# Start of a hybrid decoder step: one load for c and the bound parameters ahead of the first weight piece, and two VectorE steps moved behind the shift's columns

## The chip, the cores and the metric

The kernel runs on one core of a Trainium2 chip. The metric is the device time in microseconds (us) of one execution; a kernel's time is the median of its runs. The engines are TensorE (PE, with its weight loads as PEld), VectorE (DVE), ScalarE (ACT), GpSimd (POOL) and SyncE (SP), which here only issues DMAs.

## What is computed

One inference step of a decoder layer, for a prompt of 512 positions and 8 sample tokens (T = 520 columns), with a model width of 1024 (KO = 8 blocks of 128). What matters here is its beginning:

```
cs  = silu(c)                                  # c: 9 vectors of 1024 (1 prompt, 8 samples)
sh1, sc1, g1, sh2, sc2, g2 = split(cs @ w_mod + b_mod, 6)
h   = rmsnorm(x, norm1_g) * (1 + sc1) + sh1
u   = h @ w_in                                 # 8 groups of 1024 columns
lb, decay = functions of hg_lower and lru_lambda ("bound parameters")
```

After that follow the HGRN2 and RG-LRU recurrences over u, the gated merge, an output projection, and a second modulated norm with a feed-forward block.

## The kernel before

All matrix products run on TensorE with the weights stationary. A weight tile of 1024 x 128 is loaded as `wst`, rounded by ScalarE to the high part `whi`, and VectorE forms the low part `wlo = wst - whi`; activations `h` are kept as a high and a low part in the same way. `products` (L156) takes high x high, high x low and low x high for each block k and each half of 260 columns: six products per block, 48 per weight tile. `gemm` (L170) postpones the low weight part of the first four blocks until the fourth, so `wlo` is needed only after 16 products.

`begin` (L1718) is written out by hand and its TensorE, ScalarE and VectorE instructions keep the order in which they are written (class `InOrder`); what is issued without it is placed by a scheduler that works from a model of the times. It goes like this:

1. Loads. ScalarE's queue issues `c9` (the vectors c, L348) and `pl` (the bound parameters, L288). SyncE's queue issues the first 1 MB piece of the scale weights (`wm`, from `w_piece`), `xT0`, `pm` (`params_mod`, with b_mod and the norm gains, L1758), `xT1`, `raw` (the first three weight tiles, in four parts), `xsr`, the next piece, and so on. A load that reuses one of eight load semaphores waits for the load that had it.
2. `zeros(4)` (L1737): eight instructions of products of zeros on TensorE.
3. `cond` (L355): ScalarE's exponential of c and three VectorE steps give `cT` = silu(c). VectorE then adds 1 to two groups of columns of `pm`, starts on the bound parameters (`bounds`), ScalarE takes their exponentials and loads the table for the square root.
4. `piece(0)`: TensorE multiplies cT with the first piece; ScalarE copies the result (`modev`), TensorE turns it into columns, VectorE makes `modT`, the scale (it needs `pm`). `zeros(1)` and `zeros(3)` stand around this.
5. `high` (ScalarE) and `low` (VectorE) make the first scaled blocks of h; TensorE starts on the first three weight tiles, block by block, while three more pieces are multiplied in. The norm's root is applied afterwards: `rs` holds it per position.
6. `rooted` (L1819) multiplies each block of x by scale and root on VectorE; `evict` (L1871) multiplies a finished tile by the root on its way out of PSUM; `mod_rows` and `mod_cols` (L367, L382) multiply cT with the shift weights and give the shift's columns `shp`. From `shp` on, `high_again` and `low_again` make the final h (x with root, scale and shift), TensorE multiplies the shift into the first three tiles (`pw`), and the ordinary weight tiles begin, with the low part of their first tile made by `_split_w` (L109).

In step 6 VectorE's list reads: rooted blocks 0 to 3, the low part of the first ordinary weight tile, evict(0), rooted 4 and 5, evict(1), rooted 6 and 7, `shp`, then the low parts of h.

Of the kernel before, what the change touches and what calls it, by code (L numbers as in the profile page):

```python
# [6 lines left out]
F32 = mybir.dt.float32  # L7
# [4 lines left out]
OP = mybir.AluOpType  # L12
# [8 lines left out]
KO = D // 128  # L21
# [22 lines left out]
NM = 9  # L44
# [37 lines left out]
class Kernel:  # L82
    def __init__(self, ctx, tc, ins, outs):
        self.ctx, self.tc, self.nc = ctx, tc, tc.nc
        self.i, self.o = ins, outs
        self.start_act = self.gate_last = self.rows_last = None
        self.group, self.sigmoids, self.mod_open, self.lo_after = None, [], None, None


# [19 lines left out]
    def _split_w(self, st, place, after=None):  # L109
        if place is None:  # L110
            hi, lo = (self.wst.tile([128, KO, 128], F32R, tag="wst", name=n) for n in ("whi", "wlo"))
        else:
            pool = self.sw if place % 2 else self.whl
            hi, lo = (pool.tile([128, KO, 128], F32R, tag=f"{n}{place}", name=n, bufs=1) for n in ("whi", "wlo"))
        ins = self.nc.scalar.copy(hi, st)  # L115
        if after or self.start_act:
            self.behind(ins, after or self.start_act)
        with self.urgent():
            self.wlo = self.nc.vector.tensor_tensor(lo, st, hi.bitcast(F32), OP.subtract)  # L119
        self.whi = ins  # L120
        if self.lo_after:
            self.behind(ins, self.rounded)
            self.behind(self.wlo, self.lo_after)
            self.lo_after = None
        return hi, lo
# [156 lines left out]
    def load_parameters(self):  # L282
# [3 lines left out]
        self.gcol = self.pm[:, 70:72]  # L286
        self.pl = self.start.tile([128, 16], F32, name="pl")
        self.nc.scalar.dma_start(self.pl, self.i["params_bound"])  # L288
        self.pa = t = self.hc.tile([128, 313], F32, name="pa")
# [53 lines left out]
    def load_c(self):  # L343
        nc = self.nc
        self.act0 = self.consts.tile([1, 1], F32, name="act0")
        nc.vector.memset(self.act0, 0.0)
        self.c9 = self.start.tile([128, KO, NM], F32, name="c9")
        nc.scalar.dma_start(self.c9, self.i["c"])  # L348
        self.cT = self.hc.tile([128, KO, 32], F32, name="cT")
# [1368 lines left out]
    def begin(self):  # L1718
# [17 lines left out]

        zeros(4)  # L1737
        xsr, fs, fsh = (self.start.tile([128, KO, NB], F32, name=n) for n in ("xsr", "fs", "fsh"))
# [18 lines left out]
        self.load_x(0)  # L1757
        nc.sync.dma_start(self.pm, self.i["params_mod"])  # L1758
        self.load_x(1)
# [157 lines left out]
        rows = [load_wide("w_rows", i) for i in range(4)]  # L1917
        self.load_after = self.wide
        self.ready_w(-AHEAD, 1)
# [5 lines left out]
        evict(0)  # L1925
        rooted(4, 5)
        evict(1)
        rooted(6, 7)
        for k in range(4, KO):
            self.mod_rows(psh, k, rows[k])  # L1930
        ev = self.mod_out(psh)
        products((0,), 6, 7, tiles=(2,))
        self.mod_cols(0, self.shp[:, :, :NM], ev)
        products((1, 2), 6, 7, tiles=(2,))
        pw = pb()
# [6 lines left out]
        for i in range(KO // 2):  # L1942
# [3 lines left out]
            if i == 1:  # L1946
                nc.scalar.copy(sw, pw[:, :FIRSTS * 128])
        evict(2)
        self.last_product = nc.tensor.last
# [96 lines left out]
def layouts(i):  # L2046
# [11 lines left out]
        "xs": x[:, :, L:].transpose(1, 0, 2).reshape(128, KO * NB),  # L2058
        "c": c.T.reshape(KO, 128, NM).transpose(1, 0, 2),
        "params_mod": np.concatenate([columns(i[n]) for n in ("b_mod", "norm1_g", "norm2_g", "final_norm_g")], 1),  # L2060
        "params_bound": np.concatenate([columns(i[n]) for n in ("hg_lower", "lru_lambda")], 1),
        "params": np.concatenate([columns(i[n]) for n in ("hg_onorm_g", "lru_conv_w",
# [50 lines left out]
```

## Time and profile before

| what | us |
|---|---|
| median of 3 runs | 994.23 (993.11 to 994.47) |
| the profiled execution | 994.33 |
| its span in the trace | 992.5 |
| PE busy in the span | 979.6 |
| VectorE, ScalarE busy | 677.3, 540.2 |

The profiled execution took 994.33 us, of which the trace covers 992.5. In the timeline each line is one instruction or a run of equal ones: start, time, engine, line, operation, output<-inputs, count, and in brackets how long the engine had been idle before it and what released it. Helper lines show as L74, because the ordered engines are called through that line. PEclk is the granted TensorE clock as a share of full speed. SPq, ACTq are the issuing queues.

### The profile page before, as it was taken

How to read it: one execution, taken by the hardware profiler on the slowest of the kernel's cores; microseconds unless marked ns; L12 is line 12 of the kernel's file. 1: busy time of each engine (PE TensorE's matmuls, PEld its weight loads, DVE VectorE, ACT ScalarE, POOL GpSimd, SP SyncE). 2: the span in 40 equal slices, each digit the busy share in tenths (PEclk: the TensorE clock that was granted, in tenths of full speed). 3: DMA queues.
4: the chain of work that ended last, by engine and by line, in shares of the span. 5: the costliest groups of instructions: out<-in, count | busy, mean ns of one | idle time of the engine just before them, and what ended most of it. 6: DMA issues, size and time to landing. Idle time of an engine off the chain costs nothing.

```text
span 992.5 us, 23168 instructions
## 1 busy us (share of the span) xinstructions
PE 979.6 (99%) x9638; PEld 955.1 (96%) x9638; DVE 677.3 (68%) x1294; ACT 540.2 (54%) x1020; POOL 137.9 (14%) x252
## 2 busy tenths in 40 slices
PE   8999999999999999999999999999999999999997
PEld 6899999999999999999999999999999999999997
DVE  5884866675585658868635557767677766768685
ACT  4585746745664663456512233566456545646663
POOL 1410000000000101111100000012311331232050
PEclk8999999999999999999999999999999999999999
DMA  9653253343343425337556566322752572273242
GB/s 365 241 171 132 84 183 105 103 171 99 99 129 134 140 94 203 128 135 275 170 170 239 166 236 217 113 75 66 189 147 68 111 190 83 57 187 77 65 85 87
DMA packets 49001, 143.67 MB, mean 145 GB/s; under 512 B 6256, under 2 KB 15920, under 8 KB 47864
## 3 DMA queue, kind: packets, MB, share of 16 engines
q1 hardware_dynamic: 37008, 123.32, 36.7%
q0 software_dynamic: 11456, 18.70, 8.5%
q8 instruction: 75, 1.23, 0.5%
q14 instruction: 30, 0.25, 0.1%
q10 hardware_dynamic: 432, 0.18, 0.1%
HBM read 123.65 MB, written 11.26 MB: 136 GB/s over the span
## 4 chain that ended last, share of the span: by engine, by line
PE 92%; ACT 2%; DVE 2%; DMA 2%; issue 0%; SPq 0%; DVEq 0%; ACTq 0%
PE mm L165 62%; PE ps L1226 9%; PE pt L1226 4%; PE mm L931 2%; PE pb L1226 2%; PE pt L370 2%; PE ps L589 1%; PE ps L931 1%; PE pb L735 1%; DMA wm<-in_w_rows_dram 1%; DMA xT<-in_xT_dram 1%; PE pt L679 1%; PE pt L666 1%; PE pb L931 1%; DMA c<-in_c_dram 1%; PE mm L74 1%
## 5 line engine op out<-in xcount | busy, mean ns | idle before, releaser
L165 PE MATMUL mm<-h,whi 128*128 128x260 f32 (+1 forms) x2720 | 426.4, 285 | 0.0
L165 PEld LDWEIGHTS mm<-h,whi 128*128 128x128 f32 x2720 | 368.0, 188 | 1.6 <-issue 0.6
L119 DVE TENSOR_TENSOR wlo<-wst,whi 128x1024 fp32r<-128x1024 f32 x156 | 190.6, 1222 | 143.7 <-ACT whi L115 135.8
L165 PE MATMUL mm<-h,wlo 128*128 128x260 f32 x1360 | 255.9, 285 | 0.0
L115 ACT CAST whi<-wst 128x1024 fp32r<-128x1024 f32 x156 | 163.5, 1049 | 134.0 <-PE mm L165 106.5
L165 PEld LDWEIGHTS mm<-h,wlo 128*128 128x128 f32 x1360 | 202.1, 189 | 0.7 <-issue 0.2
L1321 POOL TENSOR_TENSOR ft<-ft,fsh 128x8 f32<-128x8 f32 x28 | 18.5, 660 | 210.3 <-DVE ft L1315 210.3
L1329 DVE TENSOR_TENSOR f<-f 128x260 f32<-128x260 f32 x64 | 27.3, 427 | 27.9 <-ACT f L1324 27.2
L1318 ACT ACTIVATE ft<-ft,fsh 128x512 f32<-128x512 f32 (+2 forms) x36 | 24.0, 675 | 36.0 <-DVE ft L1315 36.0
L244 POOL TENSOR_SCALAR ss<-ss 128x4 f32<-128x4 f32 x8 | 1.9, 233 | 284.6 <-ACT g L687 284.6
L165 PE MATMUL mm<-a,whi 128*128 128x260 f32 x256 | 37.5, 284 | 0.0
L165 PE MATMUL mm<-oa,whi 128*128 128x260 f32 x256 | 37.4, 283 | 0.0
L165 PE MATMUL mm<-b,whi 128*128 128x260 f32 x256 | 37.3, 283 | 0.0
L165 PEld LDWEIGHTS mm<-oa,whi 128*128 128x128 f32 x256 | 33.4, 188 | 0.8 <-issue 0.8
L165 PEld LDWEIGHTS mm<-a,whi 128*128 128x128 f32 x256 | 33.3, 188 | 0.8 <-issue 0.8
L165 PEld LDWEIGHTS mm<-b,whi 128*128 128x128 f32 x256 | 33.4, 188 | 0.4 <-issue 0.4
L603 DVE TENSOR_TENSOR X<-X,tb 128x512 f32<-128x512 f32 x48 | 30.9, 684 | 2.3 <-PE ps L589 1.3
L1363 POOL DMA_DIRECT2D ma<-snap x28 | 25.8, 934 | 41.9 <-issue 32.7
L1345 POOL DMA_DIRECT2D ma<-snap x28 | 26.0, 928 | 36.4 <-DMA ma<-snap 21.1
L1324 ACT ACTIVATE f<-ft 128x520 f32<-128x520 f32 (+1 forms) x36 | 20.7, 587 | 15.0 <-POOL ft L1322 13.0
L504 ACT ACTIVATE st<-st,fkq 128x128 f32<-128x128 f32 x64 | 20.0, 390 | 11.5 <-DMA st<-in_state_hgrn_dram 7.7
L192 ACT ACTIVATE gate<-pb,pa 128x260 f32<-128x260 f32 x32 | 15.4, 481 | 19.4 <-PE pb L735 19.4
(564 smaller groups left out, 2060.8 us busy)
## 6 DMA issues: line engine op xcount, KB each, us to landing
wst<-in_w_ff_dram SPq DMA_DIRECT2D x64, 512.0 KB
wst<-in_w_in_dram SPq DMA_DIRECT2D x53, 512.0 KB
wst<-in_w_mod_dram SPq DMA_DIRECT2D x32, 512.0 KB
wm<-in_w_piece_dram SPq DMA_DIRECT2D x4, 1024.0 KB
wm<-in_w_rows_dram SPq DMA_DIRECT2D x4, 1024.0 KB
st<-in_state_hgrn_dram SPq DMA_DIRECT2D x8, 512.0 KB
vb<-vd SPq DMA_DIRECT2D x8, 512.0 KB
out_dram<-st SPq DMA_DIRECT2D x8, 512.0 KB
```

The lines of the kernel that those rows point to most:

```text
L115: ins = self.nc.scalar.copy(hi, st)
L119: self.wlo = self.nc.vector.tensor_tensor(lo, st, hi.bitcast(F32), OP.subtract)
L165: self.last_product = self.nc.tensor.matmul(ps[s][:, :c.stop - c.start], x, y[:, c], start=first and n == 0, stop=last and n == 2)
L504: nc.scalar.activation(st[:, b], st[:, b], AF.Copy, scale=fkq[:, b:b + 1])
L603: last = nc.vector.tensor_tensor(half, half, factors(tbs, x, b), OP.mult)
L931: ins = nc.tensor.matmul(ps, x[:, k], self.gate_acts(j, part, k), start=j in (1, 7, 2) and k == n == 0, stop=k == 3 and n == 2, skip_group ...
L1226: ins = self.nc.tensor.matmul(ps, x[:, w], y[:, f], start=(j in (1, 7, 2) or own) and k == 0 and n == 0, stop=k == 3 and n == 2, skip_grou ...
L1318: nc.scalar.activation(t[:, :p], t[:, :p], AF.Relu, bias=sh[:, 0:1])
L1324: nc.scalar.activation(f, self.two(self.ft)[:, a:a + n], AF.Square)
L1329: self.nc.vector.tensor_tensor(f[:, n], f[:, a], f[:, b], op)
L1345: nc.gpsimd.dma_start(x[1][:, b], v[:, :n], accum_op=OP.add)
L1363: nc.gpsimd.dma_start(x[t][:, a], s[p], accum_op=OP.add)
```

## The change

c and the bound parameters become one array of 88 columns, loaded by the first DMA on SyncE's queue; `pm` moves from the third place of that queue to ScalarE's queue, as its only load there. `zeros(4)` becomes `zeros(5)`. In step 6 the low part of the first ordinary weight tile is put off until behind `shp` (in `_split_w`, `rests` holds what is put off), and `evict(1)` goes between the third and fourth pair of h's low parts.

```
-        self.pl = self.start.tile([128, 16], F32, name="pl")
-        self.nc.scalar.dma_start(self.pl, self.i["params_bound"])
+        self.nc.scalar.dma_start(self.pm, self.i["params_mod"])
...
-        self.c9 = self.start.tile([128, KO, NM], F32, name="c9")
-        nc.scalar.dma_start(self.c9, self.i["c"])
+        c = self.start.tile([128, KO * NM + 16], F32, name="c9")
+        nc.sync.dma_start(c, self.i["c"])
+        self.c9, self.pl = c[:, :KO * NM].rearrange("p (k n) -> p k n", k=KO), c[:, KO * NM:]
...
-        zeros(4)
+        zeros(5)
...
-        nc.sync.dma_start(self.pm, self.i["params_mod"])
...
+        if self.rests is not None:
+            self.whi = ins
+            self.rests.append((lo, st, hi))
+            return hi, lo
...
-        self.load_after = self.wide
+        self.load_after, self.rests = self.wide, []
...
-        rooted(4, 5)
-        evict(1)
-        rooted(6, 7)
+        rooted(4, 5, 6, 7)
...
         self.mod_cols(0, self.shp[:, :, :NM], ev)
+        for rest, st, rounded in self.rests:
+            self.wlo = nc.vector.tensor_tensor(rest, st, rounded.bitcast(F32), OP.subtract)
+        self.rests = None
...
+            if i == 2:
+                evict(1)
```

SyncE's queue at its start, before (`c9` and `pl` then stand on ScalarE's queue, in this order):

```order
L1744 DMA wm_133<-in_w_piece_dram 128x2048
L418 DMA xT0_122<-in_xT_dram 128x520
L1758 DMA pm_108<-in_params_mod_dram 128x72
L418 DMA xT1_123<-in_xT_dram 128x520
L1754 DMA raw_130<-in_w_first_dram 128x768
```

and now, with `pm` alone on ScalarE's queue:

```order
L352 DMA c9_101<-in_c_dram 128x88
L1749 DMA wm_133<-in_w_piece_dram 128x2048
L423 DMA xT0_122<-in_xT_dram 128x520
L423 DMA xT1_123<-in_xT_dram 128x520
L1759 DMA raw_130<-in_w_first_dram 128x768
```

The load of c has moved ahead of the first piece and `pm` has left the queue.

VectorE around the first scale columns, before (`ptmp`, `c8`, `c8n` belong to the bound parameters, `modT` is the scale, `fhi` the rounded first weights, `h` the low part of the first blocks):

```order
L336 SCALAR_TENSOR_TENSOR ptmp_177<-ptmp_177 128x8 x7
L74 TENSOR_TENSOR modT_107<-pt_205,pm_108 128x18
L336 SCALAR_TENSOR_TENSOR ptmp_177<-ptmp_177 128x8
L74 TENSOR_TENSOR modT_107<-modT_107,pm_108 128x18
L74 CAST fhi_131<-raw_130 128x768
L337 SCALAR_TENSOR_TENSOR ptmp_177<-ptmp_177 128x8
L339 SCALAR_TENSOR_TENSOR ptmp_177<-ptmp_177 128x8
L74 SCALAR_TENSOR_TENSOR h_157<-xT0_122,modT_107,h_156 128x512
L340 TENSOR_SCALAR c8_194<-ptmp_177 128x8
L341 TENSOR_SCALAR c8n_195<-ptmp_177 128x8
```

and now:

```order
L340 SCALAR_TENSOR_TENSOR ptmp_176<-ptmp_176 128x8 x8
L341 SCALAR_TENSOR_TENSOR ptmp_176<-ptmp_176 128x8
L343 SCALAR_TENSOR_TENSOR ptmp_176<-ptmp_176 128x8
L344 TENSOR_SCALAR c8_193<-ptmp_176 128x8
L345 TENSOR_SCALAR c8n_194<-ptmp_176 128x8
L74 TENSOR_TENSOR modT_107<-pt_204,pm_108 128x18
L74 TENSOR_TENSOR modT_107<-modT_107,pm_108 128x18
L74 CAST fhi_131<-raw_130 128x768
L74 SCALAR_TENSOR_TENSOR h_156<-xT0_122,modT_107,h_155 128x512
```

Five small steps of the bound parameters, which the scheduler had put behind the first scale step, now stand ahead of it.

VectorE around the shift's columns, before (`ma_202` and `ma_203` are the outputs of evict(0) and evict(1), `xT` with `rs` is rooted, `shp` the shift's columns):

```order
L74 SCALAR_TENSOR_TENSOR xT3_125<-xT3_125,modT_107,rs_443 128x512
L74 TENSOR_TENSOR wlo_489<-wst_486,whi_488 128x1024
L74 TENSOR_TENSOR ma_202<-mm_198,rs_443 128x520
L74 SCALAR_TENSOR_TENSOR xT4_126<-xT4_126,modT_107,rs_443 128x512
L74 SCALAR_TENSOR_TENSOR xT5_127<-xT5_127,modT_107,rs_443 128x512
L74 TENSOR_TENSOR ma_203<-mm_199,rs_443 128x520
L74 SCALAR_TENSOR_TENSOR xT6_128<-xT6_128,modT_107,rs_443 128x512
L74 SCALAR_TENSOR_TENSOR xT7_129<-xT7_129,modT_107,rs_443 128x512
L74 TENSOR_TENSOR shp_104<-pb_549,pm_108 128x2x4x9
L74 SCALAR_TENSOR_TENSOR h_157<-xT0_122,shp_104,h_156 128x512
```

and now (evict(0) and evict(1) write `ma_201` and `ma_202`), from the first eviction to the second:

```order
L74 TENSOR_TENSOR ma_201<-mm_197,rs_442 128x520
L74 SCALAR_TENSOR_TENSOR xT4_126<-xT4_126,modT_107,rs_442 128x512
L74 SCALAR_TENSOR_TENSOR xT5_127<-xT5_127,modT_107,rs_442 128x512
L74 SCALAR_TENSOR_TENSOR xT6_128<-xT6_128,modT_107,rs_442 128x512
L74 SCALAR_TENSOR_TENSOR xT7_129<-xT7_129,modT_107,rs_442 128x512
L74 TENSOR_TENSOR shp_104<-pb_546,pm_108 128x2x4x9
L74 TENSOR_TENSOR wlo_488<-wst_485,whi_487 128x1024
L74 SCALAR_TENSOR_TENSOR h_156<-xT0_122,shp_104,h_155 128x512
...
L74 SCALAR_TENSOR_TENSOR h_156<-xT5_127,shp_104,h_155 128x512
L74 TENSOR_TENSOR ma_202<-mm_198,rs_442 128x520
```

`wlo` has gone from ahead of `shp` to right behind it, and the second eviction from ahead of `shp` to behind the sixth low part of h. Behind this place the scheduler's order of the recurrences against the weight tiles differs too, through about the first fifth of TensorE's list.

More of the change, by code (lines that the diff above doesn't have):

```diff
@@ L1933, in begin @@
         self.mod_cols(0, self.shp[:, :, :NM], ev)
+        for rest, st, rounded in self.rests:
+            self.wlo = nc.vector.tensor_tensor(rest, st, rounded.bitcast(F32), OP.subtract)
+        self.rests = None
         products((1, 2), 6, 7, tiles=(2,))
@@ L2058, in layouts @@
         "xs": x[:, :, L:].transpose(1, 0, 2).reshape(128, KO * NB),
-        "c": c.T.reshape(KO, 128, NM).transpose(1, 0, 2),
+        "c": np.concatenate([c.T.reshape(KO, 128, NM).transpose(1, 0, 2).reshape(128, KO * NM),
+                             columns(i["hg_lower"]), columns(i["lru_lambda"])], 1),
         "params_mod": np.concatenate([columns(i[n]) for n in ("b_mod", "norm1_g", "norm2_g", "final_norm_g")], 1),
-        "params_bound": np.concatenate([columns(i[n]) for n in ("hg_lower", "lru_lambda")], 1),
         "params": np.concatenate([columns(i[n]) for n in ("hg_onorm_g", "lru_conv_w",
```

## Prediction

> **What bounds the kernel now.** I read the page first, then busy time by stage, then who made TensorE wait.
>
> ```profile
> span 992.5 us, 23168 instructions
> PE 979.6 (99%) x9638; PEld 955.1 (96%) x9638; DVE 677.3 (68%) x1294; ACT 540.2 (54%) x1020; POOL 137.9 (14%) x252
> ```
>
> Busy time by stage (columns: stretch, its length, then busy time and instructions of PE, PEld, DVE, ACT and POOL, granted clock, DMA share, GB/s):
>
> ```profile
> 0.00:46.74 46.74, 41.34 (x376) 33.26 (x376) 31.15 (x89) 22.71 (x43) 11.16 (x30) 0.93 0.84 322
> 42.60:46.00 3.40, 2.39 (x42) 2.17 (x44) 2.64 (x5) 0.72 (x2) 0.47 (x3) 1.00 0.35 135
> 8.00:9.00 1.00, 1.00 (x17) 0.25 (x9) 0.97 (x10) 0.77 (x3) 0.00 (x0) 0.70 0.93 380
> 15.00:16.00 1.00, 1.00 (x9) 0.95 (x8) 0.82 (x2) 0.00 (x0) 0.00 (x0) 0.88 0.94 363
> ```
>
> TensorE's waits, over the whole span:
>
> ```profile
> PE pt L74 <- DVE cT L74: 2.5, 1, 2.5
> PE pb L74 <- DVE shp L74: 2.5, 2, 1.5
> PE ps L589 <- DVE X L607: 1.1, 2, 0.7
> ```
>
> TensorE is the bound: of 992.5 us it is busy for 979.6. Of the 12.9 us that are missing, 46.74 - 41.34 = 5.4 lie ahead of the first ordinary weight tile at 46.74, which is where the change works. Whatever makes that tile start or end sooner moves everything behind it, since TensorE hardly pauses there. The two waits to attack are the one on `cT` (2.5) and the one on `shp` (2.5 in two, the longer 1.5 being the engine's start, so 1.0). Idle time isn't all: the granted clock falls inside the slice 8 to 9 (0.70 on average, so at about 8.4) and returns inside 15 to 16 (0.88, at about 15.2), and products in between are slow.
>
> The start, in order of time:
>
> ```profile
> 0.72 0.40 ACTq L74 DMA_DIRECT2D c<-in_c_dram  x1
> ...
> 1.48 3.71 PE L74 MATMUL pb<-shp 128*128 128x256 f32 x8 [1.48 <-DVE shp L74]
> ...
> 6.26 0.27 ACT L74 ACTIVATE cT<-c 128x72 f32<-128x72 f32 x1 [3.11 <-DMA c<-in_c_dram]
> 7.59 0.24 DVE L74 TENSOR_SCALAR pm<-pm 128x8 f32<-128x8 f32 x2
> 7.73 1.32 PE L74 MATMUL pt<-wm,cT 128*32 128x256 f32 x16 [2.54 <-DVE cT L74]
> 9.80 1.37 DVE L336 SCALAR_TENSOR_TENSOR ptmp<-ptmp 128x8 f32<-128x8 f32 x7
> 10.04 0.34 ACT L74 COPY modev<-pt 128x256 f32<-128x256 f32 x1
> 11.32 2.91 PE L74 MATMUL pb<-shp 128*128 128x256 f32 x6
> 11.57 0.18 DVE L74 TENSOR_TENSOR modT<-pt,pm 128x18 f32<-128x18 f32 x1 [0.40 <-PE pt L74]
> 12.00 1.34 ACT L74 ACTIVATE h<-xT,modT 128x512 fp32r<-128x512 f32 x2 [1.61 <-DVE modT L74]
> 13.66 1.43 PE L74 MATMUL mm<-h,fhi 128*128 128x260 f32 x4
> 15.29 0.63 PE L74 MATMUL mm<-h,fhi 128*128 128x260 f32 x4
> 16.09 1.07 PE L74 MATMUL pt<-wm,cT 128*32 128x256 f32 x16
> ```
>
> The chain of work that ended last has one step here, which gives c's landing at 6.17:
>
> ```profile
> 0.72 5.45 DMA c<-in_c_dram
> ```
>
> From c at 6.17 it goes to `cT`, to VectorE's steps on `pm` and the bound parameters, through ScalarE's exponentials and a table load to the copy `modev` at 10.04 (the piece itself was through by 9.05), then columns, scale, and the first products at 13.66, behind the zeros that began at 11.32.
>
> **Part 1: c first, pm on the other queue, five zeros.** Why does a load of 36 KB take 5.45 us? The packets of the slice 4 to 5, and two loads of known duration (the last column is us to landing), answer that:
>
> ```profile
> q1 hardware_dynamic: 52, 0.43, 100.4%
> q10 hardware_dynamic: 52, 0.01, 6.2%
> ```
>
> ```profile
> ma<-in_xT_dram POOLq DMA_DIRECT2D x8, 260.0 KB, 3.0
> out_dram<-hlast POOLq DMA_DIRECT2D x1, 36.0 KB, 1.9
> ```
>
> q1 carries SyncE's loads, q10 ScalarE's: 52 packets against 52, so each small packet of c waits for a big one of the first piece, and c lands when the piece does. At the head of SyncE's queue it waits for none. I bound its duration by 1.9 and 5.45 and take 3.0, the load that is seven times as large: c lands at 3.7, and `cT` is there 7.73 - 6.17 = 1.56 later, at 5.3. The first piece is issued one DMA later (0.40), and had landed with c at about 6.2: I take 6.6 (bounds: 6.2, if the later issue costs nothing, and 7.4, an estimate of three such issues). The fifth `zeros` adds two instructions of 3.71/8 = 0.46 us and ends at 6.1. So piece 0 starts at about 6.6 instead of 7.73, TensorE having paused for some 0.5 us instead of 2.5.
>
> But `pm` now stands where c stood, alone against the big packets: I let it land at 6.17, as c did (bounds: 3.7, with c; 7.4, three issues of 0.40 later). VectorE's steps on `pm` are in front of the bound parameters, whose exponentials are in front of the table load and `modev`. That stretch was 10.04 - 7.59 = 2.45 long, so `modev` comes at 6.26 + 2.45 = 8.71, 1.33 earlier. The piece is through at 7.9 and no longer decides.
>
> VectorE's five moved steps (the order in the section on the change) put 5 x 1.37/7 = 1.0 us ahead of the scale step, of which 0.40 was its idle time: `modT` gains 1.33 - 0.58 = 0.75 and ScalarE's first block starts at 11.25, ending at 11.25 + 0.67 = 11.92, the second at 12.6.
>
> Now the clock decides. The zeros start at 11.32 - 1.33 = 9.99. At full clock six take about 1.2 (half of 13.66 - 11.32), and the products start with the first block at 12.0; six take 0.8 (15.29 to 16.09), so do the next six, whose block is there at 12.6, and piece 1 starts at 13.5 (gaps 0.1 between) instead of 16.09: **2.6 gained**. At half clock the zeros cover until 13.66 - 1.33 = 12.33 and six products take 1.63 (13.66 to 15.29). The clock's return came 15.2 - 11.32 = 3.9 after dense work began, which would now be 13.9: the second six take 0.8 and piece 1 comes at 14.8, 1.3 gained; with the return at 15.2 as before it is 0.7. So **1.0 at half clock**. For the full clock speaks that TensorE had paused for 2.5 us before the fall at 8.4 and now pauses for about 0.5; and that in the stretch 42.60 to 46.00, busy for only 2.39 of 3.40, the clock stayed at 1.00. I take the full clock.
>
> Against that stands a rule of the Trainium skill (TensorE: Matmul & The Clock Gate, Part 1): the clock is decided over windows of about 3.4 us that run freely and don't start with the kernel. By it the same program gets the full clock in one run and not in another, and the sum would be rival 1's in those whose windows fall badly, whatever the pause. The trace's low stretch, 8.4 to 15.2, is two such windows and agrees; how they fall in another run, it can't show.
>
> Behind piece 1 the three rounds are TensorE's own, and all moves together. The loads move by less than the products, since their engines run full already (shares of 0.93 and 0.94 in the two slices above), but none of TensorE's waits names a load here. Were a piece late, each us of it would be a us lost.
>
> **Part 2: `wlo` and the second eviction behind `shp`.**
>
> ```profile
> 40.02 1.21 DVE L74 TENSOR_TENSOR wlo<-wst,whi 128x1024 fp32r<-128x1024 f32 x1
> 43.09 0.69 DVE L74 TENSOR_TENSOR ma<-mm,rs 128x520 f32<-128x520 f32 x1
> 45.02 0.22 DVE L74 TENSOR_TENSOR shp<-pb,pm 128x72 f32<-128x72 f32 x1
> 45.27 2.57 ACT L74 ACTIVATE h<-xT,shp 128x512 fp32r<-128x512 f32 x4 [2.72 <-DVE shp L74]
> 46.03 4.91 DVE L74 SCALAR_TENSOR_TENSOR h<-xT,shp,h 128x512 fp32r<-128x512 f32 x7 [0.79 <-ACT h L74]
> ```
>
> ```profile
> 45.30 1.52 PE L74 MATMUL pb<-raw,shp 128*32 128x128 f32 x48 [1.01 <-DVE shp L74]
> 46.74 2.17 PE L165 MATMUL mm<-h,whi 128*128 128x260 f32 x14
> 48.75 0.73 PE L1959 MATMUL pt<-pick,shw 128*128 128x9 f32 x6
> 50.62 0.65 PE L165 MATMUL mm<-h,whi 128*128 128x260 f32 x4
> 53.49 0.77 PE L165 MATMUL mm<-h,whi 128*128 128x260 f32 x5
> ```
>
> On before's clock: `shp` loses 1.21 + 0.69 = 1.9 us of work ahead of it, and could stand at 43.1 to 43.3. TensorE is then late: it had waited 1.01 and is free at 44.29. So `pw` starts at 44.29 and the tile at 45.73, 1.01 sooner, not 1.9. What was moved now lies ahead of the tile's operands. `wlo` ends at about 44.7 and the first low part of h starts then (46.03 before); one takes 4.91/7 = 0.70, so the sixth ends at 48.9, the eviction of 0.69 follows, and the seventh and eighth end at about 50.4 and 51.1. The tile needs 48 products of (53.49 - 50.62)/24 = 0.12 and the 0.73 of the shift's transposes: 45.73 + 5.76 + 0.73 = 52.2, if nothing waits. Its seventh block starts about 50.8 and its eighth at 51.5, so both low parts are just there; `wlo`, needed after 16 products, has 2 us in hand. Before, the tile ended at 53.49: its first 14 products took 2.17 instead of 1.7, waiting for low parts. **1.3 gained** (0.8, if the moved eviction holds the seventh block, to 1.7).
>
> Evict(1) now frees its PSUM buffer at 49.6, and the second ordinary tile wants it at 52.2. Beyond those 2.6 us, each us late would be a us of the kernel.
>
> **The sum**, against the profiled execution's 994.33 (the median is 994.23, the same within 0.1): 994.33 - 2.6 - 1.3 = **990.4**.
>
> **Rivals.**
> 1. *The clock is at half when the products start.* Part 1 gives 1.0 instead of 2.6: 992.0. For it: the first zeros were 3.7 us long when the clock was found full, not much less than the 4.6 of now, the piece may land at 7.4 and leave a pause of 1.3, and around `modev` TensorE pauses again. The skill's free windows would bring about this case.
> 2. *c isn't what it hangs on.* If `pm` lands at 7.4, `modev` stays at 9.9 and the two loads have only changed places: 994.33 - 1.3 = 993.0. Against it: c, in the place where `pm` is now, landed at 6.17.
> 3. *Slower:* TensorE's list through the recurrences is ordered differently, and later low parts may let the products of the recurrences (L589, five levels for each of four pairs of heads, 20 groups) wait for VectorE. L607 shows two waits, the longest 0.7. At 0.5 in each group it is 10 us against the 3.9 gained: 1000.4; from 0.3 a group (6 us) the kernel is slower than before by 0.2%. Against it: VectorE is busy for only 677.3 of 992.5, and only two groups wait on L607 now.
> 4. *Better:* `pm` lands with c. Then `modev` follows the piece at about 7.5, the scale, behind VectorE's small steps, at 11.57 + 0.58 - 2.5 = 9.7, piece 1 comes at 12.3: 3.8, and with part 2 at its best of 1.7 it is 988.8.
>
> **Chances.** The forecast 0.56, rival 1 0.24, rival 2 0.10, rival 3 0.03, rival 4 0.07. The range reaches from rival 4 to rival 1 with its smaller gain (0.7 and, in part 2, 0.8): 988.7 to 992.8. Outside lie most of rival 2 and rival 3, and a little of each other. A measurement of this kernel tells 0.2%, 2.0 us, from no change: faster is under 992.2. That takes the forecast, rival 4 and two thirds of rival 1 (0.79); same takes the last third and rival 2 (0.18); slower is rival 3 (0.03).
>
> **What would show it.** Right: c's exponential at 3.7 to 4.2, piece 0 at 6.2 to 6.9, `modev` at about 8.7, piece 1 at about 13.5 and no granted clock under 1 between 8.5 and 13; TensorE without a wait on `shp`, and `pw` to the end of the first tile about 0.3 shorter. Wrong in part 1: `modev` still near 10 with VectorE idle ahead of its steps on `pm`, or a clock of 0.5 at 12. Wrong in part 2: TensorE waiting for h's seventh low part. Wrong altogether: more than 3 us of waits at L594 (L589 before).

## The result, and the profile after

The changed kernel takes 994.48 us (median of 22 runs, 992.64 to 996.47) beside 993.28 us for the kernel before on the same chip (22 runs, 991.24 to 995.57). The ratio is 1.0015, with a 95% interval of 1.0008 to 1.0022: slower by some 1.5 us, where 3.9 us of gain were forecast, and above the range's end of 992.8. The profiled execution took 995.73 us:

```profile
span 994.0 us, 23170 instructions
PE 981.1 (99%) x9640; PEld 956.9 (96%) x9640; DVE 677.5 (68%) x1294; ACT 541.4 (54%) x1020; POOL 136.8 (14%) x252
```

Line numbers behind the edits are five higher than before: the products of a tile are L170 (L165), those of the recurrences L594 (L589), and the X products of VectorE L612 (L607).

**The start gained more than forecast.** The chain that ended last gives c's load, and the timeline the steps that the prediction priced:

```profile
0.72 1.98 DMA c<-in_c_dram
```

```profile
2.79 0.27 ACT L74 ACTIVATE cT<-c 128x72 f32<-128x72 f32 x1
4.12 0.24 DVE L74 TENSOR_SCALAR pm<-pm 128x8 f32<-128x8 f32 x2
6.28 1.61 PE L74 MATMUL pt<-wm,cT 128*32 128x256 f32 x16 [0.17 <-DVE ptmp L338]
7.96 0.37 ACT L74 COPY modev<-pt 128x256 f32<-128x256 f32 x1 [1.29 <-PE pt L74]
8.85 1.54 PE L74 MATMUL pb<-shp 128*128 128x256 f32 x6
11.93 1.07 PE L74 MATMUL pt<-wm,cT 128*32 128x256 f32 x16
39.77 1.52 PE L74 MATMUL pb<-raw,shp 128*32 128x128 f32 x48
48.41 2.08 PE L170 MATMUL mm<-h,whi 128*128 128x260 f32 x16
```

Piece 1 starts at 11.93 instead of 16.09, the shift's products no longer wait for `shp`, and the second ordinary tile starts at 48.41 instead of 53.49: 5.1 us ahead of the profiled execution of before.

**Then it was lost between 100 and 500 us.** These are the sums of two tables by stage over that stretch, of the kernel before and of the changed one (first number the length, then TensorE's busy time):

```profile
sum 400.00, PE 398.37 PEld 388.63 DVE 276.59 ACT 231.47 POOL 27.27; mean PE 49.80 PEld 48.58 DVE 34.57 ACT 28.93 POOL 3.41
```

```profile
sum 400.00, PE 394.79 PEld 385.12 DVE 271.54 ACT 228.08 POOL 27.26; mean PE 49.35 PEld 48.14 DVE 33.94 ACT 28.51 POOL 3.41
```

TensorE is idle for 3.6 us more. This is also where the order differs: TensorE's lists in the two traces are alike only from about 430 us on, behind half of their instructions and not behind a fifth, as the section on the change has it. Behind 500 us both kernels keep it busy throughout until 980. TensorE's waits in the changed kernel:

```profile
PE ps L594 <- DVE X L612: 4.5, 4, 1.7
PE mm L170 <- DVE X L475: 0.7, 1, 0.7
PE mm L170 <- POOL h L74: 0.3, 1, 0.3
```

Before, the first of these was 1.1 in two. And idle time isn't the whole loss: the granted clock (third number from the end) falls to half behind two of the waits, which it did nowhere in this stretch before.

```profile
275.00:280.00 5.00, 3.37 (x46) 3.33 (x47) 5.00 (x11) 3.12 (x5) 0.00 (x0) 0.71 0.38 105
370.00:375.00 5.00, 3.42 (x76) 3.30 (x77) 5.00 (x12) 2.19 (x4) 0.62 (x1) 0.77 0.20 76
375.00:380.00 5.00, 5.00 (x96) 4.82 (x96) 3.73 (x8) 0.64 (x1) 2.14 (x4) 0.89 0.75 233
```

With the slice behind the first of these (0.95) the shortfalls add to 5 x (0.29 + 0.05 + 0.23 + 0.11) = 3.4 us. So 5.1 gained, 3.6 lost to waits and 3.4 to the clock make 1.9 us of loss in these two executions; their spans differ by 994.0 - 992.5 = 1.5.

**What TensorE waits for** is seen at the third and the fourth start of a recurrence (the level of one step, L589 here, then the level of two, L594, which needs the four X products of L612):

```profile
270.88 1.10 PE L589 MATMUL ps<-X 128*32 128x64 f32 x64
271.78 1.28 ACT L781 ACT_TABLE_LOAD   x1
271.94 0.75 DVE L612 TENSOR_TENSOR X<-X,ma 128x256 f32<-128x256 f32 x2
273.62 1.03 ACT L116 CAST whi<-wst 128x1024 fp32r<-128x1024 f32 x1
274.68 1.23 DVE L124 TENSOR_TENSOR wlo<-wst,whi 128x1024 fp32r<-128x1024 f32 x1 [1.98 <-ACT whi L116]
275.82 0.75 DVE L612 TENSOR_TENSOR X<-X,ma 128x256 f32<-128x256 f32 x2
276.63 0.46 PE L594 MATMUL ps<-X 128*32 128x32 f32 x32 [1.67 <-DVE X L612]
...
370.04 1.22 DVE L789 TENSOR_TENSOR_SCAN hs<-ag,gate 128x512 f32<-128x512 f32 x1
371.23 0.75 DVE L612 TENSOR_TENSOR X<-X,ma 128x256 f32<-128x256 f32 x2
372.04 0.46 PE L594 MATMUL ps<-X 128*32 128x32 f32 x32 [1.31 <-DVE X L612]
372.43 3.65 PE L170 MATMUL mm<-h,whi 128*128 128x260 f32 x16
```

At the third start the next tile's `wlo` stands in VectorE's list between the first two and the last two X products. It needs ScalarE's `whi`, which stands behind a table load and one activation, so VectorE is idle for 1.98 us with work behind it that is ready, and TensorE waits for that work. At the fourth start a scan stands there. The 16 products at 372.43 take 3.65 us where the same 16 took 2.08 at 48.41: that is the half clock.

The kernel before has waiting rows too. At its third start:

```profile
277.63 1.22 DVE L119 TENSOR_TENSOR wlo<-wst,whi 128x1024 fp32r<-128x1024 f32 x1 [2.19 <-ACT whi L115]
278.77 0.75 DVE L607 TENSOR_TENSOR X<-X,ma 128x256 f32<-128x256 f32 x2
279.67 0.70 DVE L798 SCALAR_TENSOR_TENSOR y<-y 128x520 f32<-128x520 f32 x1
280.29 0.75 DVE L607 TENSOR_TENSOR X<-X,ma 128x256 f32<-128x256 f32 x2
281.10 0.46 PE L589 MATMUL ps<-X 128*32 128x32 f32 x32 [0.68 <-DVE X L607]
```

There a `wlo` that waits for 2.19 us stands ahead of all four X products, and between them only a y operation; TensorE waits for 0.68. At its fourth start a scan, a `wlo` that need not wait and two small products stand between them, and TensorE waits for 0.41. So it isn't enough that something stands there: what it costs depends on how long it waits, and on the products that TensorE's list still has ahead of the need.

### The profile page after: what moved, and what is told of

It reads as the page before. It is cut to its first block, busy times and chain, and to the rows that moved or that the text cites. A ratio compares the mean times of both kernels' runs of the same rounds, so it can differ in the third digit from the quotient of the medians.

```text
span 994.0 us, 23170 instructions
## 1 busy us (share of the span) xinstructions
PE 981.1 (99%) x9640; PEld 956.9 (96%) x9640; DVE 677.5 (68%) x1294; ACT 541.4 (54%) x1020; POOL 136.8 (14%) x252
## 4 chain that ended last, share of the span: by engine, by line
PE 91%; ACT 4%; DVE 4%; issue 1%; POOL 0%; DMA 0%; DVEq 0%; ACTq 0%; POOLq 0%
PE mm L170 59%; PE ps L1231 9%; PE pt L1231 4%; PE mm L936 2%; PE pb L1231 2%; PE pt L375 2%; PE mm L74 1%; PE ps L936 1%; PE pb L740 1%; PE ps L594 1%; PE ps L74 1%; PE pt L74 1%; PE pt L671 1%; PE pt L684 1%; DVE wlo L124 1%; ACT whi L116 1%
## 5 line engine op out<-in xcount | busy, mean ns | idle before, releaser
L170 PE MATMUL mm<-h,whi 128*128 128x260 f32 (+1 forms) x2720 | 427.9, 286 | 1.0 <-DVE X L475 0.7
L170 PEld LDWEIGHTS mm<-h,whi 128*128 128x128 f32 x2720 | 370.0, 190 | 2.4 <-PE mm L170 0.9
L170 PE MATMUL mm<-h,wlo 128*128 128x260 f32 x1360 | 258.0, 286 | 0.0
L170 PEld LDWEIGHTS mm<-h,wlo 128*128 128x128 f32 x1360 | 203.3, 190 | 1.1 <-issue 0.6
L170 PE MATMUL mm<-a,whi 128*128 128x260 f32 x256 | 37.5, 284 | 0.0
L170 PE MATMUL mm<-oa,whi 128*128 128x260 f32 x256 | 37.4, 283 | 0.0
L170 PE MATMUL mm<-b,whi 128*128 128x260 f32 x256 | 37.3, 283 | 0.0
L608 DVE TENSOR_TENSOR X<-X,tb 128x512 f32<-128x512 f32 x48 | 30.8, 683 | 6.8 <-PE ps L594 4.1
L170 PEld LDWEIGHTS mm<-oa,whi 128*128 128x128 f32 x256 | 33.4, 188 | 0.8 <-issue 0.8
L170 PEld LDWEIGHTS mm<-a,whi 128*128 128x128 f32 x256 | 33.3, 188 | 0.8 <-issue 0.8
L170 PEld LDWEIGHTS mm<-b,whi 128*128 128x128 f32 x256 | 33.4, 188 | 0.4 <-issue 0.4
L509 ACT ACTIVATE st<-st,fkq 128x128 f32<-128x128 f32 x64 | 20.3, 391 | 17.1 <-DMA st<-in_state_hgrn_dram 13.9
```

The lines of the kernel that those rows point to most:

```text
L170: self.last_product = self.nc.tensor.matmul(ps[s][:, :c.stop - c.start], x, y[:, c], start=first and n == 0, stop=last and n == 2)
L608: last = nc.vector.tensor_tensor(half, half, factors(tbs, x, b), OP.mult)
```

## The experiments

The theory: the start gains what the trace shows, and the loss is the order in which the scheduler put VectorE's list through the recurrences once the first tiles came out differently. The rivals: the earlier loads or the moved instructions cost something later by themselves; or the clock falls by chance.

Ratios are to runs of the kernel before on the same chip, whose medians were 992.88 (e1 to e4), 993.15 (e5 to e8) and 993.38 (e9 to e12).

| run | start | order behind the first tiles | us | ratio, 95% interval |
|---|---|---|---|---|
| the change | new | new | 994.48 | 1.0015 (1.0008 to 1.0022) |
| e1 | part 1 | free | 992.94 | 0.9995 (0.9986 to 1.0004) |
| e2 | part 2 | free | 997.04 | 1.0040 (1.0025 to 1.0054) |
| e3 | new | before's | 989.62 | 0.9968 (0.9957 to 0.9980) |
| e4 | before | new | 998.18 | 1.0054 (1.0039 to 1.0070) |
| e5 | new | new, X products together | 990.12 | 0.9964 (0.9949 to 0.9979) |
| e6 | part 1 | before's | 992.05 | 0.9991 (0.9980 to 1.0001) |
| e7 | part 2 | before's | 993.20 | 0.9998 (0.9986 to 1.0010) |
| e8 | new | free, with two rules | 1007.45 | 1.0135 (1.0113 to 1.0157) |
| e9 | new | before's, X products together | 989.20 | 0.9957 (0.9944 to 0.9970) |
| e10 | new | as e5, q's product moved too | 989.43 | 0.9962 (0.9947 to 0.9976) |
| e11 | new, zeros(4) | before's | 990.81 | 0.9977 (0.9966 to 0.9987) |
| e12 | new, `pm` on SyncE | before's | 993.13 | 0.9996 (0.9985 to 1.0007) |

**Order or start? e3 and e4.** Everything that is emitted behind the last eviction of the first tiles is the same in both kernels, instruction by instruction. So a list of the order in one kernel can be laid on the other, as ordering rules without a wait:

```
-        Kernel(ctx, tc, ins, outs).run()
+        k = Kernel(ctx, tc, ins, outs)
+        k.run()
+        keep(tc, nc, k.mark)
...
+def keep(tc, nc, mark):
...
+    for order in ORDER.values():
+        last = None
...
+                ins = nc.get_inst_by_name(f"I-{first + k}")
+                if last:
+                    tc.add_manual_dep(ins, last, NOSYNC, reason="order")
+                last = ins.name
```

(`mark` is the first instruction behind the first tiles. ORDER has one list for each engine: before's for e3, the changed kernel's for e4.)

> The changed kernel whole, but from the end of the first tiles on (everything emitted behind the last eviction) each engine's instructions are held in the order in which the kernel before has them. Theory (order): the 5.1 us that the first ordinary tile is ahead stay to the end, 993.3 - 5.1 = 988.2 us, 987 to 989.5, with waits for X L612 near the 1.1 us of before. Rival A: no order can help, 993.5 to 995. Rival B: 988 to 994 at random with the granted clock.

> The kernel before whole, but from the end of the first tiles on each engine's instructions are held in the order in which the changed kernel has them; loads, zeros and the first tiles as before. Theory (order): it has the loss without the gain, 993.3 + 3.6 of waits + 2 to 3.4 of clock = 999 to 1000.3 us, with some 4.5 us of waits for X L612. Rival A (the cost lies in the moved loads and instructions, not in the order): 993.3. Rival B: 992 to 995.

Measured: e3 989.62, e4 998.18. The same sums over 100 to 500 us, of e3 and of e4:

```profile
sum 400.00, PE 398.37 PEld 388.81 DVE 274.86 ACT 230.74 POOL 27.31; mean PE 132.79 PEld 129.60 DVE 91.62 ACT 76.91 POOL 9.10
```

```profile
sum 400.00, PE 394.88 PEld 385.20 DVE 273.62 ACT 230.55 POOL 27.33; mean PE 131.63 PEld 128.40 DVE 91.21 ACT 76.85 POOL 9.11
```

The busy time goes with the order, not with the start: 398.37 with before's order, as in the kernel before, and 394.88 with the new one, as in the changed kernel (394.79). The new order alone costs 0.54%, the new start alone brings 0.32%, and 1.0054 x 0.9968 = 1.0022 is close to the 1.0015 of both. The rival that the moved instructions cost by themselves falls with e3, and chance with both: the medians follow the order, up and down. e3 came out 1.4 us above its theory's 988.2, just outside the range, mostly because the 5.1 was taken from one profile of before, whose start was a slow one (the last parts of this section come back to it); e4 stayed 0.8 under its range's 999, with 1.7 us of clock lost in its profile instead of 3.4.

**What in the order? e5.** The changed kernel held in its own order but for four instructions. At the third start, for instance, VectorE's list reads

```
 TENSOR_TENSOR X_645<-X_645,ma 128x256 x2
-TENSOR_TENSOR wlo<-wst,whi 128x1024
 TENSOR_TENSOR X_645<-X_645,ma 128x256 x2
+TENSOR_TENSOR wlo<-wst,whi 128x1024
```

> The changed kernel with every instruction of every engine held in its own order behind the first tiles, but for four instructions of VectorE: at each recurrence start the four X products now stand next to each other, and what stood between them (a y operation at the second start, the next tile's wlo at the third, a scan and an eight column product at the fourth) stands behind them. Theory (the waits come from what stands between these products): of the 4.5 us that TensorE waited for X L612, 0.7, 1.7 and 1.3 go and about 0.8 at the fourth start stay; with them most of the half clock windows behind them go (0 to 3.4 us in a run): 994.4 - 3.7 - 1 = 989.7 us, 988.7 to 991. Rival (the order as a whole, with TensorE's groups standing too early): at most 1 us of the waits goes, 993 to 994.5.

Measured: 990.12. In its trace, the third start and the waits that are left:

```profile
271.07 1.43 DVE L612 TENSOR_TENSOR X<-X,ma 128x256 f32<-128x256 f32 x4
273.65 0.76 PE L594 MATMUL ps<-X 128*32 128x32 f32 x64
273.81 1.23 DVE L124 TENSOR_TENSOR wlo<-wst,whi 128x1024 fp32r<-128x1024 f32 x1 [1.32 <-ACT whi L116]
```

```profile
PE ps L594 <- DVE X L608: 0.9, 2, 0.6
PE ps L594 <- DVE X L612: 0.8, 1, 0.8
```

TensorE doesn't wait at the third start at all, and `wlo` starts as soon behind its `whi` as it did (1.06 us behind the start of `whi` in both): it had only held up others. Four instructions, each moved behind two X products, take the ratio from 1.0015 to 0.9964, some 5 us; the wait for X L612 falls from 4.5 to 0.8, though 0.9 for X L608 is new, and the clock stays at 1.00 in every slice of 100 to 500 us. This is the cause, shown by itself. The measured time is 0.4 us from the theory's 989.7; of the rival's 993 to 994.5 nothing is left.

**A rule in place of a list: e8.** Can the scheduler be told?

```
+            if b == 1:
+                self.behind(self.wlo, last)
...
-            nc.vector.tensor_tensor_scan(hs[:, :L], a[:, :L], g[:, :L], 0.0, OP.mult, OP.add)
+            self.scans.append(nc.vector.tensor_tensor_scan(hs[:, :L], a[:, :L], g[:, :L], 0.0, OP.mult, OP.add))
...
-            if b == 1 and hs[1] < H - 1:
-                for ins in self.scans:
+            if b == 1:
+                for ins in self.scans if hs[1] < H - 1 else self.scans[1::2]:
```

> The changed kernel, order free again, with two rules for the scheduler: the latest wlo made by then and, at the last recurrence, the two scans stand behind the last of the four X products. In the order that comes out one y operation alone stands between the products at the second, third and fourth start. Theory: waits for X L612 of about 2 us in place of 4.5, 988.7 to 991. Rival (the rule moves the wait elsewhere, for instance to the products that need the wlo): 992.5 to 994.5.

Measured: 1007.45, by far the slowest; the expectation failed and the rival's kind of thing happened. Its second start:

```profile
184.57 1.10 PE L589 MATMUL ps<-X 128*32 128x64 f32 x64
186.09 1.23 DVE L124 TENSOR_TENSOR wlo<-wst,whi 128x1024 fp32r<-128x1024 f32 x1 [2.19 <-ACT whi L116]
187.23 0.76 DVE L612 TENSOR_TENSOR X<-X,ma 128x256 f32<-128x256 f32 x2
188.14 0.46 PE L594 MATMUL ps<-X 128*32 128x32 f32 x32 [2.47 <-ACT y L804]
```

The rule keeps `wlo` out from between the X products, and now one stands ahead of all four, again waiting for its `whi`, so the group of products waits 2.47 us (the profile puts that down to ScalarE's y, but the first X products end at 187.99 too). The kernel before has that same order at its third start, shown above, and lost 0.68 by it. There TensorE has 20 products of a weight tile left between the two levels of the recurrence; in e8, where TensorE's list differs too, L594 follows L589 at once. Over 100 to 500 us TensorE is idle for 13.9 us (5.2 in the changed kernel), and the mean clock of the run is 0.988 (0.997). It is the same mechanism, with nothing left to cover the wait: a rule fixes one place, and the scheduler makes the rest of the order anew.

**The two parts apart: e1, e2, e6, e7.** Each part of the change alone, first with a free order, then with before's order held. In e1 and e6 part 2 is taken back:

```
-        self.load_after, self.rests = self.wide, []
+        self.load_after = self.wide
...
-        rooted(4, 5, 6, 7)
+        rooted(4, 5)
+        evict(1)
+        rooted(6, 7)
...
-        for rest, st, rounded in self.rests:
-            self.wlo = nc.vector.tensor_tensor(rest, st, rounded.bitcast(F32), OP.subtract)
-        self.rests = None
...
-            if i == 2:
-                evict(1)
```

and in e2 and e7 part 1:

```
-        self.nc.scalar.dma_start(self.pm, self.i["params_mod"])
+        self.pl = self.start.tile([128, 16], F32, name="pl")
+        self.nc.scalar.dma_start(self.pl, self.i["params_bound"])
...
-        c = self.start.tile([128, KO * NM + 16], F32, name="c9")
-        nc.sync.dma_start(c, self.i["c"])
...
+        self.c9 = self.start.tile([128, KO, NM], F32, name="c9")
+        nc.scalar.dma_start(self.c9, self.i["c"])
...
-        zeros(5)
+        zeros(4)
...
+        nc.sync.dma_start(self.pm, self.i["params_mod"])
```

> Part 1 alone: c and the bounds as one load at the head of SyncE's queue, the modulation parameters on ScalarE's queue, five products of zeros; the second eviction and the next tile's low part stand where they stood before. Theory (the start gains, and the scheduler's other order of the recurrences gives it back): in this kernel the twelve rows of VectorE between the four recurrence starts read as in the kernel before (at the third start the four X products have one y operation between them and no wlo), so the 4.2 us that piece 1 came earlier should stay: 993.3 - 4.2 = 989.1 us, 988 to 990.5, and TensorE should wait for X L612 for about 1 us in all. Rival A (the earlier loads and the moved parts themselves cost something later, whatever the order): the loss shows here too, 992.5 to 994.5. Rival B (granted clock that falls in any long run, by chance): within 0.7 us of the kernel before plus or minus, 990 to 993, with no wait at X L612 that differs.

> Part 2 alone: the second eviction behind the third samples part and the next tile's low part behind the shift's columns; the loads and four products of zeros as before. Here VectorE's rows at the third recurrence start read as in the changed kernel: the next tile's wlo stands between the first two and the last two X products. Theory (order): about 0.9 us gained by the end of the first ordinary tile, then 3.6 us of TensorE idle more than before and 2 to 3.4 us of lost clock: 993.3 - 0.9 + 6 = 998, 996 to 999.5, with about 4.5 us of waits for X L612. Rival A (the moved loads cost): 992.4, as part 1 is not in it. Rival B (chance of the clock): 992 to 994.

> Part 1 alone, with the order behind the first tiles held as the kernel before has it. In the free run of part 1 the next tile's rounding waited 2.15 us for its weights' landing and VectorE held the shift's columns until then, so TensorE waited 3.00 us. Theory (part 1 alone is eaten by that load): the tile behind the first one starts 1.2 us earlier than in the profile of before, 992.9 - 1.2 = 991.7 us, 990.7 to 993. Rival (what part 1 lost was the order): with the old order held it keeps the 4.2 us, 988.5 to 990.

> Part 2 alone, with the order behind the first tiles held as the kernel before has it. Theory (the parts work together: part 2 takes the wait for the weights away from the shift's columns, part 1 brings everything ahead of them forward): free of the new order's 5 us it is faster than before by 1.0 to 2.7 us, 990.2 to 991.9, and the whole change with the same order, 989.6, is ahead of it by what part 1 brings. Rival (part 2 itself costs something later): not faster than before, 992.5 to 997.

Measured: e1 992.94, e2 997.04, e6 992.05, e7 993.20. e2 came out as the theory had it: the bad order comes with part 2, and the waits for X L612 are again 4.4 us. For e1 the theory failed: it has the good order, waits for X L612 for 1.1 us only, and still gained nothing that can be told; 992.94 lies in the ranges of both rivals, and it is the earlier start itself that costs something, though not later but at the first tile. Its trace says why:

```profile
36.36 1.04 ACT L74 CAST whi<-wst 128x1024 fp32r<-128x1024 f32 x1 [2.15 <-DMA wst<-in_w_in_dram]
37.44 1.22 DVE L74 TENSOR_TENSOR wlo<-wst,whi 128x1024 fp32r<-128x1024 f32 x1 [1.90 <-ACT whi L74]
42.72 2.45 PE L74 MATMUL pb<-raw,shp 128*32 128x128 f32 x48 [3.00 <-DVE shp L74]
```

With the products earlier, the weights of the first ordinary tile are late, `wlo` holds VectorE until they are there, and `shp` stands behind `wlo`. Part 2 takes `wlo` away from there. So the parts aren't a sum: with the order held, part 1 alone gives 0.09% (not told from nothing), part 2 alone 0.02%, both 0.32%. e6 came out as its theory had it; e7 as its rival, though not for the rival's reason: nothing is lost later (TensorE waits for X L612 for 1.1 us, as before), there is only little to gain while piece 1 is late. Its second tile starts at 52.38, and e4's, with before's whole start, at 52.89. (One of e7's twelve runs took 3355.55 us; why stays open, and the median hardly feels it.)

**The start itself: e11 and e12**, both with before's order held, to be compared with e3's 989.62 (0.9968; e3 ran on another chip, so the ratios compare better than the medians).

```
-        zeros(5)
+        zeros(4)
```

> The changed kernel with the old order held (989.6 us), but four products of zeros at the start in place of five. TensorE then stands idle for about 1.2 us ahead of the first piece in place of 0.3. Theory (an idle stretch of 2.2 us or more there is what brought half speed for the products from 7.5 to 14 us; 1.35 us did not in part 2's profile): no change, 989.3 to 990. Rival (any gap ahead of the first piece brings half speed): 2.1 to 2.8 us more, 991.7 to 992.4, with the first piece at 1.9 us in place of 1.07.

```
-        self.nc.scalar.dma_start(self.pm, self.i["params_mod"])
...
         self.load_x(0)
+        nc.sync.dma_start(self.pm, self.i["params_mod"])
```

> The changed kernel with the old order held (989.6 us), but the modulation parameters are loaded from SyncE's queue behind the first x piece, as before, and not from ScalarE's. Before, VectorE's first operation on them ran at 7.59 us. Theory (they are needed for the modulation at 8.7 to 9.1 us only): no change, 989.3 to 990. Rival (they land late, and the first products wait): 0.5 to 3 us more.

Measured: e11 990.81, e12 993.13. Both theories had "no change", and both failed. Of e12, the timeline:

```profile
7.24 0.24 DVE L74 TENSOR_SCALAR pm<-pm 128x8 f32<-128x8 f32 x2 [3.21 <-DMA pm<-in_params_mod_dram]
7.79 0.49 ACT L74 ACTIVATE ptmp<-ptmp 128x8 f32<-128x8 f32 x2 [4.90 <-DVE ptmp L74]
...
9.71 0.34 ACT L74 COPY modev<-pt 128x256 f32<-128x256 f32 x1
10.10 0.61 PE L74 MATMUL pt<-pick,modev 128*128 128x9 f32 x4 [1.91 <-ACT modev L74]
```

c is as early as in the change, and it helps little: VectorE waits for `pm`, the bound parameters stand behind it on VectorE, their exponentials and the table load behind those, and `modev` behind the table load. What e12's expectation overlooked is that modulation isn't the first user of `pm`. In this profile the second tile starts at 50.58 instead of e3's 48.84, 1.7 us later, and its run of 991.45 is one of five from 991.35 to 991.62; three others lie at 993.0 to 993.3 and four at 994.7 to 994.8, and what slows those stays open. By the ratios 0.9996 - 0.9968 = 0.28% is gone, nearly all of the 0.32% that the change gains with this order. So `pm` on the other queue carries part 1, and c's place without it brings nothing that can be told (0.9996).

e11's median fell between its theory and its rival: five of twelve runs lie from 989.39 to 990.11, like e3, five from 990.79 to 991.31 and two at 993.1. Its profiled run is slow from the first piece on:

```profile
6.51 1.93 PE L74 MATMUL pt<-wm,cT 128*32 128x256 f32 x16 [1.26 <-DVE ptmp L338]
10.11 2.91 PE L74 MATMUL pb<-shp 128*128 128x256 f32 x6
```

In the change these took 1.61 and 1.54, in e2, behind a gap of 1.35, the piece took 1.07. The theory was that the idle stretch brings the half speed. The durations say otherwise: TensorE's first eight zeros took 3.78 us here, 0.47 each, where six at full speed took 1.54, 0.26 each. So TensorE ran at half speed from its first product, as it did in every profile of this case (3.65 to 3.78 for eight zeros, 4.19 to 4.64 for ten), and in e11's it hadn't left it by 13 us; in e2's it had by 6.47. That the gap decides when it leaves is suggested by the runs and not shown by the traces. The fifth product of zeros shortens the gap to 0.2 to 0.8 us (the profiles with five), e11 differs from e3 in it alone, and the runs of e3, of e5 and of e9 each lie within 1.2 us, where those of the kernel before spread over more than 4 in each set.

**The best: e9 and e10.** The same idea carried on: e9 moves a y operation, a scan, two small products and a `wlo` behind the X products in before's order; e10 adds one move to e5. The first of e9's moves, and e10's:

```
 TENSOR_TENSOR X_645<-X_645,ma 128x256 x2
-SCALAR_TENSOR_TENSOR y<-y 128x520
 TENSOR_TENSOR X_645<-X_645,ma 128x256 x2
+SCALAR_TENSOR_TENSOR y<-y 128x520
...
-TENSOR_TENSOR y<-y,hs 128x520
 TENSOR_TENSOR X_646<-mm,X_646 128x520
+TENSOR_TENSOR y<-y,hs 128x520
```

> The changed kernel with the order of the kernel before held behind the first tiles, and in it the four X products next to each other at the third start (a y operation moved behind them) and at the fourth (a scan, two eight column products and the next tile's wlo moved behind them). The same kernel without these moves took 989.6 us and waited 1.1 us for X L612. Theory (what stands between the products makes the waits): 0.6 to 1.1 us of these waits go, 988.6 to 989.1 us. Rival (in the old order these moves only shift the wait to a later product): 989.4 to 990.5.

> The changed kernel in its own order with the four X products together at each start (990.1 us before this step), and one more move on VectorE: at about 120 us the product that reads TensorE's bank for q stands ahead of the y product that it stood behind; TensorE waited 0.7 us for it there. Theory: 0.6 us less, 989.5, 989.1 to 989.9. Rival (the bank is freed by something else too): 990.1.

Measured: e9 989.20, e10 989.43. e10 came out as its theory had it, and its trace agrees: the 0.7 us of waits for X L475 is gone. e9 lies between its theory's range and its rival's, and its trace shows the rival: the waits for X L612, 1.1 us in e3, are gone, but those for X L608 rise from 0.2 to 1.2, and over 100 to 500 us TensorE is busy for 398.38 us as against e3's 398.37. What its profile is ahead of e3's comes in part from the start, where its second tile begins at 48.36 and e3's at 48.84; the moves themselves gained nothing there that shows. The steps (0.4 and 0.7 us in the medians, each between different chips) are small against the ratios' intervals; e9's 0.9957 is the lowest of all, and it beats both kernels.

## Why the prediction was wrong

1. **c's load.** Forecast to take 3.0 us, measured 1.98. The lower bound, the nearest row in size (36 KB, 1.9), was the right one to take; the row seven times as large was not. The Trainium skill (DMA: Bandwidth & Descriptors, Anatomy of one DMA — SWDGE (gpsimd) path) fits a fixed part of about 2.0 us to loads that GpSimd issues. This one, of 44 KB from SyncE's queue, took 1.98, which agrees.
2. **`pm` was thought to land at 6.17** and to cost half of the gain. It was there by 4.12, when VectorE had done with `cT` and took its first step on it without a wait, so rival 4 is what happened in part 1. Rival 2's mechanism was rightly seen, `modev` does hang on `pm`: e12 shows it with `pm` at 7.24 and `modev` at 9.71.
3. **The clock at the start.** The forecast of full clock was right (six products of zeros in 1.54 us). But the 2.6, measured as 4.2, was set against one execution of before in which the clock was at half there; in e2, with before's loads, piece 1 came at 13.28. The gain of part 1 is 1.4 us against such a start and 4.2 against the profiled one. The profiled 994.33 lies 1.1 above the later median of 993.28, so the base of the sum was partly a bad draw. The prediction also took the clock for full until 8.4, as recorded. But the eight zeros of 3.71 us, with which rival 1 argues, are 0.46 each where the six of the change took 0.26: TensorE began at half speed there too. e3's gain of 3.3 us in the medians is what the start is worth.
4. **Part 2.** Forecast 1.3: from piece 1 to the second tile it took 53.49 - 16.09 = 37.40 before and 48.41 - 11.93 = 36.48 now, 0.9 gained. The wait of 1.01 on `shp` went as forecast. The stretch from `pw` to the tile's end, which was to be 0.3 shorter, became longer: 48.41 - 39.77 = 8.64 against 53.49 - 45.30 = 8.19. Of that 0.3 is the wait for GpSimd's part for the samples, which the prediction hadn't looked at. What it missed is that the parts need each other (e6 and e7).
5. **The step that failed** is the sentence that whatever makes the first tile end sooner moves everything behind it, "since TensorE hardly pauses there", and the weight of 0.03 on rival 3. Its place was right (L594 waiting for VectorE) and so was the sign by which it would be known, more than 3 us of waits at L594. Of its cause it had a part: at the third start it was a low part that stood later in VectorE's list than before, but what it held up by waiting was ready work behind it, and at the other two starts it was a y operation and a scan. Its price was wrong: it counted 20 groups at equal waits, and it was four waits of 4.5 us together, at three of the four starts alone, with up to 3.4 us of clock on top. The kernel's order isn't a given that a time shift leaves alone. The lists of both kernels could be compared before any run, row by row: `wlo` between the two pairs of X products at the third start stood there to be read, and L607 was the wait that the profile of before already showed. What it would cost the lists alone don't say, since before's list too has a `wlo` among these products, at its fourth start.

## What to carry to other kernels

Where a scheduler plans the order, compare its lists over the whole kernel and not only around the edit, and look in each in-order engine's list for an instruction that waits for another engine and stands ahead of work that the busiest engine needs, and then how much that engine has left to do before it needs it. To tell an edit's own effect from that of the order that came with it, lay the order of one kernel on the other, both ways: here it split 1.0015 into 0.9968 and 1.0054 in one pair of runs. And read a start from more than one execution, or from the row's duration at full clock, before pricing what an edit of it gains.

## What the chip showed

- **Short waits can cost twice.** In the changed kernel's profile, behind waits of 1.67 us, and of 0.83 and 1.31 us within 2 us, the granted clock went to half:

```profile
277.00:278.00 1.00, 1.00 (x16) 0.98 (x5) 1.00 (x3) 0.50 (x1) 0.00 (x0) 0.54 0.88 180
278.00:279.00 1.00, 1.00 (x6) 1.00 (x6) 1.00 (x3) 0.23 (x1) 0.00 (x0) 0.50 0.77 315
279.00:280.00 1.00, 1.00 (x7) 1.00 (x6) 1.00 (x4) 0.41 (x1) 0.00 (x0) 0.50 0.00 0
280.00:281.00 1.00, 1.00 (x8) 1.00 (x8) 1.00 (x4) 0.00 (x0) 0.00 (x0) 0.75 0.00 0
```

  (0.46 + 0.50 + 0.50 + 0.25) / 0.50 = 3.4 us of it, while TensorE was busy throughout. The Trainium skill (TensorE: Matmul & The Clock Gate, Part 1) has windows of about 3.4 us that run freely, and the length agrees. The same page of the Trainium skill advises to avoid gaps over about 3 us (Why this matters for your kernels). No wait in this stretch was longer than 1.67, so here the measurement decides. With most of these waits gone, in e5, no slice of 5 us from 100 to 500 us is under 1.00.
- **It varies from run to run.** The same waits (4.4 to 4.5 us) cost 3.4 us of clock in the changed kernel's profile, 1.7 in e4's and none in e2's, whose profiled run took 994.16 us where the median is 997.04. Of the changed kernel's runs the two with a mean clock of 1.000 took 992.64 and 993.45 us, the four with 0.995 took 995.62 to 996.47. But the kernel before, without these waits, has runs from 0.992 to 1.000 too, so a run's mean alone doesn't say where its clock was lost.
- **The granted clock doesn't show all half speed.** In e11's profile the first piece took 1.93 us and the six products of zeros 2.91, as long as at half clock before, with the clock recorded at full (1.00 in the slice from 5 to 10 us too):

```profile
10.00:15.00 5.00, 5.00 (x20) 4.36 (x19) 3.72 (x7) 2.39 (x4) 1.38 (x3) 1.00 1.01 407
```

  The same holds for the zeros at TensorE's start, at about 0.46 us each and a recorded 1.00 in every profile. The durations decide. Why the record misses it stays open.
